# A hybrid layer on one core: attention blocks turned by row halves, reciprocals spread behind the values, and two small moves around the MLP

## The chip, the cores and the metric

The kernel runs on one core of a Trainium2 chip. A core has a matrix engine (PE, whose weight loads the profile lists apart as PEld), a vector engine (DVE), a scalar engine (ACT), a general engine (POOL), a queue engine (SP) that starts the transfers, and 16 DMA engines. Matrix products read from the on-chip memory of 128 partitions and write to eight banks of a second memory (PSUM), from which DVE and ACT copy results away. The metric is device time in microseconds of one execution, the median of several runs.

## The reference

One layer of a decoder on an input of 1024 positions and 1024 features, in float32. After a norm, one input projection feeds two mixers side by side: a gated delta rule (four heads of 128, chunks of 64) and a dilated attention (eight heads of 64). Their outputs go through one output projection and are added to the input. A norm, an up projection to 2 × 2816 columns, a causal convolution of width 3, a gate, a down projection and a final norm follow. Of the attention:

```python
def band_attention(q, k, v, n_back):          # query l sees keys l-n_back..l
    ...
    s = jnp.einsum('...nqd,...nkd->...nqk', qb, kk)
    ...
    m = jnp.max(s, axis=-1)
    p = jnp.exp(s - m[..., None])
    den = jnp.sum(p, axis=-1)
    num = jnp.einsum('...nqk,...nkd->...nqd', p, vv)

def dilated_attention(q, k, v):
    for window, dil in ((128, 1), (512, 4), (2048, 16)):
        ...                                   # band attention over the keys at stride dil
    ...
    num_tot = wts[0][..., None] * nums[0] + wts[1][..., None] * nums[1] + wts[2][..., None] * nums[2]
    out = num_tot / den_tot[..., None]
```

and of the end of the layer:

```python
    h = rmsnorm(x, norm2_w)
    u = causal_dwconv(h @ w_up, ffn_conv_w)
    gate, up = u[..., :D_FF], u[..., D_FF:]
    x = x + (jax.nn.silu(gate) * up) @ w_down
    ...
    return rmsnorm(x, final_norm_w)
```

## The kernel before

Large products are made of three products of a rounded high part and a low part (`mm3`: high·high, low·high, high·low); in the rows they are `xhi,whi`, `xlo,whi`, `xhi,wlo`, each 128 x 512. The up and down projections are made of seven products instead of eight blocks (`P1` to `P7` in `up`), on sums and differences of the operands' blocks.

**Order of the work.** The kernel is written as generators, one for each strand: the norm and gates, the dense input projection, eight chains of the delta rule, the attention, the output projection, the MLP. A planner (`Weave`, lines 46 to 118) runs them in turn. It keeps an estimated time of PE and of when each tile is ready; a strand yields how long it would have to wait (`need`), and another strand's products are put in its place. What comes out is one fixed order of all PE instructions, which is stamped on them. The order on DVE and ACT is made by a scheduler from the program order and two priorities: `uv` and `ua` are the urgent handles of DVE and ACT, `ve` and `ac` the plain ones. So a product of the attention stands between products of the dense projection, and where its operand is late, PE waits, whatever could be done behind it.

**The attention** (lines 892 to 1045) takes two heads at a time (`e` = 0, 1, in partitions 0 to 63 and 64 to 127), four head pairs `pi`, two halves `hh` of the positions, and in each half two pairs of 128-row blocks (`u` = 0, 1 and 2, 3). The function `advance` does one such pair a step: it turns the pair before, computes this pair's scores, and finishes the pair before.

- `scores` (line 904): products of `kT,qT`, by row halves for the near keys (64*128) and in sixteenths for the dilated ones (64*32), into banks `asc` and `atr`, two of each. `softmax` (929): DVE takes maximum and mask into `sm`, ACT the exponential with its sum `den`.
- `turn` (942): DVE writes `rd`, the reciprocal of `den` over 128 x 128. Then each 128 x 128 block of `sm` is transposed on PE (`tp`, line 192, `ps<-ident,sm` with L193), for each head into one bank of `asc` or `atr`. DVE copies the near blocks to `pt`, ACT the dilated ones to `pb`. The next scores use the same banks.
- `spread` (966): PE transposes the two `rd` of a pair into a bank, so that the reciprocals lie along the free dimension. At the end of a half ACT copies the bank to `rT`.
- `values` (975): `pt,vn`, by column halves (128*64). `merge_classes` (984): `pb,vc` for the dilated keys. `give` (998): DVE multiplies the bank of values by `rT` into `oT`, and SP sends it to the mixer's memory.

In the rows an entry such as 64*128 is the part of the 128 x 128 array that an instruction uses, rows by columns.

**The passage to the up projection** (`up`, lines 1246 to 1288, for the first column block, where `before is None`). PE computes P1, P5, three quarters of P2, P6, the last quarter of P2; then `rms2_power` (1174) sums the squares of the second norm with `ones` and has DVE and POOL make the reciprocal roots `rs`; then P7, then `rms2_spread` (1183): eight transpositions of `rs` into two banks, copied by DVE to `rstdB`; then P4. ACT copies the banks of P1, P6 and P7 to `p1`, `u2`, `u3` (rows `p<-pa`, `u<-pa`), beside splitting weights (`S`, `pair`).

**The last product** (`last_product` 1485, `complete` 1421, `final_norm` 1430). The last rows of the down projection end in two halves of 256 columns. For each, DVE adds to `x1h`, ACT squares it, DVE adds the square to `rstdB`; then PE sums `rstdB` over the partitions with `ones`, POOL makes the reciprocal root, PE spreads it, DVE scales and SP writes out.

Of the kernel before, what the change touches and what calls it, by code (L numbers as in the profile page):

```python
# [15 lines left out]
P = 128  # L16
# [128 lines left out]
def hybrid_layer(tc, I, out):  # L145
# [43 lines left out]
        tc.stamp_issue_order_token(nc.tensor.matmul(dst, lhs, rhs, start=start, stop=stop, **kw).ins, TOKEN)  # L189
        wv.product(us, dst, lhs, rhs)  # L190

    def tp(dst, src):
        tc.stamp_issue_order_token(nc.tensor.transpose(dst, src, ident).ins, TOKEN)  # L193
        wv.product(0.11, dst, src)

    def mm3(dst, lhs, rhs, first, last, **kw):
        us = 0.2135 * rhs[0].shape[-1] / 512
# [694 lines left out]
    def attention():  # L892
# [47 lines left out]
            it["den"] = den  # L940

        def turn(pair):
            pts = A("pt", "dv*", shape=(P, 4, 256))
            for b, (it, tag) in enumerate(zip(pair, ("asc", "atr"))):
                sm, near, far, den, u = it["sm"], it["near"], it["far"], it["den"], it["u"]
                rd = tile_(sp, [P, P], F32, "rd", ("r0", "r1", "w0", "w1")[u], 1)
                uv.reciprocal(rd.rearrange("p (e d) -> p e d", e=2), den[:, :, None].to_broadcast([P, 2, 64]))
                it["rd"] = rd
                nf = -(-far // P)
                it["pt"] = []  # L950
                for e in range(2):
                    pt = pts[:, 2 * b + e, :]
                    it["pt"].append(pt)
                    pp = bank(tag)
                    yield wv.need(pp, sm, slack=TSLACK[b])
                    for i in range(near // P):
                        tp(pp[:, i * P:(i + 1) * P], sm[:, e, far + i * P:far + (i + 1) * P])
                    for i in range(nf):
                        tp(pp[:, near + i * P:near + (i + 1) * P], sm[:, e, i * P:(i + 1) * P])
                    uv.tensor_copy(pt[:, :near], pp[:, :near])  # L960
                    for i in range(nf):
                        rows = min(far - i * P, P)
                        ua.activation(it["pb"][e][:rows, it["u"], i, :], pp[:rows, near + i * P:near + (i + 1) * P],
                                      AF.Copy)

        def spread(pair):
            g = pair[0]["g"]
# [5 lines left out]
                ac.activation(g["rT"], g["rb"], AF.Copy)  # L973

        def values(pair):
            yield wv.need(pair[0]["po"], *pair[0]["pt"], slack=-PSLACK)
            for it in pair:
                u = it["u"]
                for i in range(it["near"] // P):
                    for e, er in enumerate(HALVES):  # L980
                        mm(it["po"][er, u * P:(u + 1) * P], v8(it["vn"])[:, it["k0"] // P + i, er],
                           it["pt"][e][:, i * P:(i + 1) * P], 0.11, u == 0 and i == 0, False, skip_group_check=True)

        def merge_classes(g):
            vcv = g["vc"].rearrange("p (b c d) -> p b c d", b=2, c=4)
            po, hh = g["po"], g["hh"]
            yield wv.need(*g["pb"], slack=-PSLACK)


            parts = (((0, 128, 0), (1, 64, 2)) if hh else ((0, 64, 2),))  # L990
            for b, rows, u in parts:
                for c in range(4):
                    for e, er in enumerate(HALVES):
                        mm(po[er].rearrange("p (u t) -> p u t", u=4)[:, u:, 32 * c:32 * c + 32],
                           vcv[:rows, b, c, er], g["pb"][e][:rows, u:, b, 32 * c:32 * c + 32], 0.11 - 0.028 * u,
                           False, c == 3 and b == hh, skip_group_check=True)

        def give(g):
# [14 lines left out]
        def advance(pair):  # L1013
            done = pipe.pop() if pipe else None
            if done is not None:
                yield from turn(done)
            if pair is not None:
                yield from scores(pair)
                pipe.append(pair)
            if done is not None:  # L1020
                yield from spread(done)
                yield from values(done)
                if done[1]["u"] == 3:
                    yield from merge_classes(done[0]["g"])
                    give(done[0]["g"])

        for pi in range(4):
            q, k, vn, vc = cur
            for hh in range(2):
                if hh == 1 and pi < 3:  # L1030
                    yield from wv.until(("a", pi + 1, 1))
                    cur = att_load(pi + 1)
                po = bank("ch")
                pb = [A("pb", "qa", shape=(P, 4, 1 + hh, P)) for _ in range(2)]
                if pi == 3 and hh == 1:
                    wv.done.add("last group")
                for t in pb:
                    for rows, b in (((slice(96, 128), 0), (slice(32, 64), 1)) if hh else ((slice(32, 64), 0),)):
                        po_.memset(t[rows, 0 if b < hh else 2, b, :], 0.0)
# [206 lines left out]
    def up(n, before):  # L1246

        xg, xu = A("xg", "kT"), A("xu", "kT")
        pa = bank("asc", "pa")
        yield from up_product(n, "P1", pa, True, False)  # L1250
        p1 = tile_(sp, [P, 512], F32, "p1", "t2", 2)
        ac.activation(p1, pa, AF.Copy)
        if before is not None:
            yield from before()
        pc = bank("ch", "pc")
        if before is None:

            yield from up_product(n, "P5", pc, True, False)
            pd = bank("hf", "pd")
            yield from up_product(n, "P2", pd, ks=range(3))  # L1260
        yield from up_product(n, "P6", pa, False, False)
        u2 = tile_(wp, [P, 512], F32, "u2", "wlo", 2)
        ac.activation(u2, pa, AF.Copy)
        if before is None:
            yield from up_product(n, "P2", pd, False, ks=(3,))
            rs = rms2_power()
        else:
            yield from up_product(n, "P5", pc, True, False)
        yield from up_product(n, "P7", pa, False, False)
        if before is None:  # L1270
            rms2_spread(rs)
        else:
            pd = yield from next_bank("hf")
            yield from up_product(n, "P2", pd)
        u3 = tile_(sp, [P, 512], F32, "u3", "t2", 2)
        ac.activation(u3, pa, AF.Copy)
        ve.tensor_tensor(xu[:, half(1)], u3, pc, op=OP.add)
        ve.tensor_tensor(xg[:, half(0)], p1, pd, op=OP.add)
        yield from up_product(n, "P4", pa, False, True)
        ac.activation(xu[:, half(0)], pa, AF.Copy)  # L1280

        def rest():
            yield from up_product(n, "P3", pc, False)
            ve.tensor_tensor(xg[:, half(1)], u2, pc, op=OP.add)
            del W[n]
            up_tail(n, xg, xu)
        ve.tensor_tensor(xu, xu, rstdB, op=OP.mult)
        last["rest"] = rest
# [129 lines left out]
        x = x1h[m][:, part(m, hh, sl)]  # L1418
        ve.tensor_tensor(x, x, pd[:, sl], op=OP.add)

    def complete(m, hh, sl):

        sp_ = part(m, hh, sl)
        x = x1h[m][:, sp_]
        sq = tile_(sp, [P, 512], F32, "sq3", "t2", 2)
        ac.activation(sq[:, sl] if m else rstdB[:, sp_], x, AF.Square)
        if m:
            ve.tensor_tensor(rstdB[:, sp_], rstdB[:, sp_], sq[:, sl], op=OP.add)

# [24 lines left out]
    def mlp_down():  # L1454
# [117 lines left out]
```

## Time and profile before

| | |
|---|---|
| median of 3 runs | 1228.7 us (1227.79 to 1230.6) |
| the profiled execution | 1227.88 us |
| its span in the trace | 1226.0 us |
| PE busy | 1205.9 us, 98% |
| PEld busy | 992.4 us, 81% |
| DVE busy | 948.6 us, 77% |
| ACT busy | 574.7 us, 47% |
| POOL busy | 53.2 us, 4% |
| `ps<-ident,sm` on PE | 184 instructions, 23.9 us |
| `ps<-pt,vn` / `ps<-pb,vc` on PE | 240, 16.6 us / 192, 9.6 us |

A row of a group reads: line, engine, operation, tiles (output, then operands), shape in the array and form, count; then busy us, mean ns of one; then the idle time of the engine just before them and what ended it. Matrix products overlap, so the start of one to the start of the next is the time that it takes, and the duration of one is longer than that. In rows in order of time the first number is the start in the span, the second the length of the row's work together, and the count stands at the end. Line 189 is the helper of all products, 193 that of all transpositions, 139 and 141 those of the plain and the urgent instructions of DVE and ACT; so groups are told apart by their tiles.

### The profile page before, as it was taken

To read this page: it belongs to the slowest core of one execution; us is meant where nothing else is said; L and a number is where in the kernel's file an instruction comes from. 1 tells how busy PE (TensorE), PEld (TensorE's weight loads), DVE (VectorE), ACT (ScalarE), POOL (GpSimd) and SP (SyncE) were. 2 spreads that over 40 slices of the span, in tenths; PEclk is the share of its full clock that TensorE was granted. 3 is DMA by queue.
4 is the path that set the end of the run, shared out by engine and by line. 5 is a ranking of instruction groups with operands and counts; after the bars stand their busy time and mean duration, and the time that the engine had idled before them with its cause. 6 is when DMAs were issued, how large, how long until landed. Compare 5 with 4: busy or idle time off the path is not lost.

```text
span 1226.0 us, 17889 instructions
## 1 busy us (share of the span) xinstructions
PE 1205.9 (98%) x6880; PEld 992.4 (81%) x6880; DVE 948.6 (77%) x1458; ACT 574.7 (47%) x1123; POOL 53.2 (4%) x58
## 2 busy tenths in 40 slices
PE   9999999999999999999999999999999999999996
PEld 7878887888777777788788888888888888787886
DVE  7675964566477686667888989889888889898875
ACT  7393344256344453555545445444454453344441
POOL 0211010003100000000000000000000000000000
PEclk9999999999999999999999999999999999999998
DMA  7425252345733213444123132231322397455623
GB/s 232 104 87 157 84 152 74 121 137 151 225 104 113 80 36 89 165 151 152 52 88 103 52 103 82 74 103 52 103 88 68 122 366 256 166 168 172 193 86 138
DMA packets 85799, 154.79 MB, mean 126 GB/s; under 512 B 21169, under 2 KB 36305, under 8 KB 85713
## 3 DMA queue, kind: packets, MB, share of 16 engines
q1 hardware_dynamic: 85712, 153.64, 39.0%
q8 instruction: 54, 0.88, 0.3%
q14 instruction: 33, 0.26, 0.1%
HBM read 117.68 MB, written 35.93 MB: 125 GB/s over the span
## 4 chain that ended last, share of the span: by engine, by line
PE 82%; DVE 8%; DMA 4%; issue 2%; ACT 2%; POOL 0%; SPq 0%; POOLq 0%; DVEq 0%; ACTq 0%
PE ps L189 43%; PE pa L189 19%; PE pc L189 10%; PE dw L189 8%; PE ps L193 3%; DMA wd<-in_wd 2%; DVE pr L139 2%; DVE x1h L139 1%; DVE wd L139 1%; DVE kT L139 1%; ACT dec L139 1%; DMA xt<-in_xT 1%; DVE wlo L139 0%; DMA wst<-in_wu 0%; DVE r L139 0%
## 5 line engine op out<-in xcount | busy, mean ns | idle before, releaser
L189 PE MATMUL dw<-pr 128*128 128x512 f32 (+1 forms) x984 | 213.4, 377 | 2.9 <-DVE x1h L139 2.5
L189 PEld LDWEIGHTS dw<-pr 128*128 128x128 f32 x984 | 176.0, 188 | 39.2 <-DVE x1h L139 4.7
L189 PE MATMUL ps<-xhi,whi 128*128 128x512 f32 x384 | 158.6, 413 | 0.0
L189 PE MATMUL ps<-xlo,whi 128*128 128x512 f32 x384 | 149.9, 390 | 0.4 <-DVE xlo L139 0.4
L189 PE MATMUL ps<-xhi,wlo 128*128 128x512 f32 x384 | 150.3, 391 | 0.0
L189 PE MATMUL pa<-T,pair 128*128 128x512 f32 x528 | 127.1, 389 | 0.6 <-ACT u L139 0.6
L189 PEld LDWEIGHTS pa<-T,pair 128*128 128x128 f32 x528 | 98.9, 188 | 21.1 <-ACT u L139 0.6
L189 PEld LDWEIGHTS ps<-xhi,wlo 128*128 128x128 f32 x384 | 72.0, 188 | 15.8 <-DVE wlo L139 0.2
L189 PEld LDWEIGHTS ps<-xhi,whi 128*128 128x128 f32 x384 | 72.3, 188 | 15.2 <-issue 2.6
L189 PEld LDWEIGHTS ps<-xlo,whi 128*128 128x128 f32 x384 | 72.4, 189 | 12.5 <-DVE xlo L139 0.8
L139 ACT ACTIVATE whi<-wst 128x1024 fp32r<-128x1024 f32 (+2 forms) x42 | 43.0, 1023 | 82.0 <-PE ps L189 68.1
L139 ACT ACTIVATE u<-pa 128x512 f32<-128x512 f32 x44 | 26.3, 599 | 110.6 <-PE pa L189 110.6
L139 DVE SCALAR_TENSOR_TENSOR y<-xu,fcw,y 128x1023 f32<-128x1023 f32 (+1 forms) x44 | 56.4, 1281 | 25.7 <-ACT y L139 25.6
L189 PE MATMUL pa<-B,A 128*128 128x512 f32 x264 | 63.4, 389 | 0.0
L189 PE MATMUL pa<-T,S 128*128 128x512 f32 x264 | 63.4, 389 | 0.0
L189 PE MATMUL pc<-B,pair 128*128 128x512 f32 x264 | 63.4, 389 | 0.0
L189 PE MATMUL pc<-T,S 128*128 128x512 f32 x264 | 63.4, 389 | 0.0
L139 DVE TENSOR_TENSOR wst<-wst 128x512 f32<-128x512 f32 x88 | 60.5, 687 | 0.8
L189 PE MATMUL ps<-B,pair 128*128 128x512 f32 x252 | 60.5, 389 | 0.0
L139 DVE TENSOR_TENSOR wlo<-wst,whi 128x1024 fp32r<-128x1024 f32 (+2 forms) x42 | 49.4, 1177 | 13.6 <-ACT whi L139 13.5
L139 ACT ACTIVATE pr<-wd 128x1024 fp32r<-128x1024 f32 x33 | 34.9, 1059 | 50.7 <-DVE wd L139 24.8
L141 ACT ACTIVATE sm<-sm,mx 128x128 f32<-128x128 f32 (+7 forms) x64 | 35.5, 557 | 48.1 <-DVE mx L141 48.1
(240 smaller groups left out, 2371.0 us busy)
## 6 DMA issues: line engine op xcount, KB each, us to landing
wst<-in_wu SPq DMA_DIRECT2D x44, 512.0 KB, 3.7
wd<-in_wd SPq DMA_DIRECT2D x44, 512.0 KB, 4.0
upark<-y SPq DMA_DIRECT2D x22, 512.0 KB, 3.7
wst<-in_wi SPq DMA_DIRECT2D x21, 512.0 KB, 3.7
r<-upark SPq DMA_DIRECT2D x11, 512.0 KB, 7.9
r<-upark SPq DMA_DIRECT2D x22, 256.0 KB, 7.2
wa<-in_wd SPq DMA_DIRECT2D x22, 256.0 KB, 2.7
wst<-in_wv SPq DMA_DIRECT2D x8, 512.0 KB, 3.6
```

The costliest lines, as they stand in the source:

```text
L139: return getattr(eng, op)(*a, **kw)
L141: return getattr(eng, op)(*a, **kw)
L189: tc.stamp_issue_order_token(nc.tensor.matmul(dst, lhs, rhs, start=start, stop=stop, **kw).ins, TOKEN)
L193: tc.stamp_issue_order_token(nc.tensor.transpose(dst, src, ident).ins, TOKEN)
```

## The change

There are four parts.

1. `turn` transposes each 128 x 128 block in two pieces, one for each half of the rows (64 partitions by 128 columns), with the 64 x 64 identity of the same rows. The piece of the upper rows goes to one bank and that of the lower rows to another. 184 transpositions in 128*128 become 368 in 64*128. A bank now holds both heads of one row half; a copy takes the near blocks of both heads for one row half (`pt`), or one dilated block of both heads (`pb`). There are as many copies as before. `pb` is laid out anew, with 12 memsets by POOL instead of 24. The reciprocal `rd` is written behind the copies in the program.
2. In `advance`, `values` and `merge_classes` come ahead of `spread`, and `give` is last. With it the copy `rT` comes later on ACT.
3. In the first `up`, the bank copies `p1`, `u2`, `u3` are urgent instructions of ACT, and `rms2_spread` moves from between P7 and P4 to behind P4.
4. In the last half of the last product, the square of the last row block isn't added to `rstdB` by DVE; PE sums it as a second product into the same bank.

```diff
-    def tp(dst, src):
-        tc.stamp_issue_order_token(nc.tensor.transpose(dst, src, ident).ins, TOKEN)
-        wv.product(0.11, dst, src)
+    def tp(dst, src, idt=None, us=0.11):
+        tc.stamp_issue_order_token(nc.tensor.transpose(dst, src, ident if idt is None else idt).ins, TOKEN)
+        wv.product(us, dst, src)
...
         def turn(pair):
-            pts = A("pt", "dv*", shape=(P, 4, 256))
+            pts = A("pt", "dv*", shape=(P, 2, 2, 256))
             for b, (it, tag) in enumerate(zip(pair, ("asc", "atr"))):
-                sm, near, far, den, u = it["sm"], it["near"], it["far"], it["den"], it["u"]
-                rd = tile_(sp, [P, P], F32, "rd", ("r0", "r1", "w0", "w1")[u], 1)
+                sm, near, far, u, den = it["sm"], it["near"], it["far"], it["u"], it["den"]
+                nn, nf = near // P, -(-far // P)
+                pt = it["pt"] = pts[:, b]
+                pps = [bank(tag) for _ in range(2)]
+                yield wv.need(*pps, sm, slack=TSLACK[b])
+                pvs = [pp.rearrange("p (e i t) -> p e i t", e=2, t=64) for pp in pps]
+                for e in range(2):
+                    for i in range(nn + nf):
+                        o = far + i * P if i < nn else (i - nn) * P
+                        for pv, rr in zip(pvs, HALVES):
+                            tp(pv[:, e, i, :], sm[rr, e, o:o + P], ident[rr, rr], 0.055)
+                for pv, rr in zip(pvs, HALVES):
+                    uv.tensor_copy(pt.rearrange("p e (i t) -> p e i t", t=P)[:, :, :nn, rr], pv[:, :, :nn, :])
+                    for i in range(nf):
+                        rows = min(it["far"] - i * P, P)
+                        ua.activation(it["pb"][i][:rows, :, u, rr], pv[:rows, :, nn + i, :], AF.Copy)
+                rd = it["rd"] = tile_(sp, [P, P], F32, "rd", ("r0", "r1", "w0", "w1")[u], 1)
                 uv.reciprocal(rd.rearrange("p (e d) -> p e d", e=2), den[:, :, None].to_broadcast([P, 2, 64]))
-                it["rd"] = rd
-                nf = -(-far // P)
-                it["pt"] = []
-                for e in range(2):
-                    pt = pts[:, 2 * b + e, :]
-                    it["pt"].append(pt)
-                    pp = bank(tag)
-                    yield wv.need(pp, sm, slack=TSLACK[b])
-                    for i in range(near // P):
-                        tp(pp[:, i * P:(i + 1) * P], sm[:, e, far + i * P:far + (i + 1) * P])
-                    for i in range(nf):
-                        tp(pp[:, near + i * P:near + (i + 1) * P], sm[:, e, i * P:(i + 1) * P])
-                    uv.tensor_copy(pt[:, :near], pp[:, :near])
-                    for i in range(nf):
-                        rows = min(far - i * P, P)
-                        ua.activation(it["pb"][e][:rows, it["u"], i, :], pp[:rows, near + i * P:near + (i + 1) * P],
-                                      AF.Copy)
...
             if done is not None:
-                yield from spread(done)
                 yield from values(done)
                 if done[1]["u"] == 3:
                     yield from merge_classes(done[0]["g"])
+                yield from spread(done)
+                if done[1]["u"] == 3:
                     give(done[0]["g"])
...
-                pb = [A("pb", "qa", shape=(P, 4, 1 + hh, P)) for _ in range(2)]
+                pb = [A("pb", "qa", shape=(P, 2, 4, P)) for _ in range(1 + hh)]
...
-        ac.activation(p1, pa, AF.Copy)
+        copy = (ua if before is None else ac).activation
+        copy(p1, pa, AF.Copy)
...
-        ac.activation(u2, pa, AF.Copy)
+        copy(u2, pa, AF.Copy)
...
         yield from up_product(n, "P7", pa, False, False)
-        if before is None:
-            rms2_spread(rs)
-        else:
+        if before is not None:
...
-        ac.activation(u3, pa, AF.Copy)
+        copy(u3, pa, AF.Copy)
...
         yield from up_product(n, "P4", pa, False, True)
         ac.activation(xu[:, half(0)], pa, AF.Copy)
+        if before is None:
+            rms2_spread(rs)
...
+    squares = {}
...
-    def complete(m, hh, sl):
+    def complete(m, hh, sl, apart=False):
...
-        if m:
+        if apart:
+            squares["last"] = sq
+        elif m:
             ve.tensor_tensor(rstdB[:, sp_], rstdB[:, sp_], sq[:, sl], op=OP.add)
...
-            mm(ss[:, c:c + 1], rstdB[:, o:o + P], ones[:, :1], 0.215)
+            more = squares.get("last")
+            mm(ss[:, c:c + 1], rstdB[:, o:o + P], ones[:, :1], 0.215, True, more is None)
+            if more is not None:
+                mm(ss[:, c:c + 1], more[:, sl.start + c * P:sl.start + c * P + P], ones[:, :1], 0.215, False, True)
...
-            complete(4 + i, 0, sl)
+            complete(4 + i, 0, sl, sl.start > 0 and i == 3)
```

More of the change, by code (lines that the diff above doesn't have):

```diff
@@ L975, in values @@
         def values(pair):
-            yield wv.need(pair[0]["po"], *pair[0]["pt"], slack=-PSLACK)
+            yield wv.need(pair[0]["po"], pair[0]["pt"], slack=-PSLACK)
             for it in pair:
@@ L981, in values @@
                         mm(it["po"][er, u * P:(u + 1) * P], v8(it["vn"])[:, it["k0"] // P + i, er],
-                           it["pt"][e][:, i * P:(i + 1) * P], 0.11, u == 0 and i == 0, False, skip_group_check=True)
+                           it["pt"][:, e, i * P:(i + 1) * P], 0.11, u == 0 and i == 0, False, skip_group_check=True)
         def merge_classes(g):
@@ L994, in merge_classes @@
                         mm(po[er].rearrange("p (u t) -> p u t", u=4)[:, u:, 32 * c:32 * c + 32],
-                           vcv[:rows, b, c, er], g["pb"][e][:rows, u:, b, 32 * c:32 * c + 32], 0.11 - 0.028 * u,
+                           vcv[:rows, b, c, er], g["pb"][b][:rows, e, u:, 32 * c:32 * c + 32], 0.11 - 0.028 * u,
                            False, c == 3 and b == hh, skip_group_check=True)
@@ L1033, in attention @@
                 po = bank("ch")
-                pb = [A("pb", "qa", shape=(P, 4, 1 + hh, P)) for _ in range(2)]
+                pb = [A("pb", "qa", shape=(P, 2, 4, P)) for _ in range(1 + hh)]
                 if pi == 3 and hh == 1:
                     wv.done.add("last group")
-                for t in pb:
-                    for rows, b in (((slice(96, 128), 0), (slice(32, 64), 1)) if hh else ((slice(32, 64), 0),)):
-                        po_.memset(t[rows, 0 if b < hh else 2, b, :], 0.0)
+                for rows, b in (((slice(96, 128), 0), (slice(32, 64), 1)) if hh else ((slice(32, 64), 0),)):
+                    po_.memset(pb[b][rows, :, 0 if b < hh else 2, :], 0.0)
                 g = dict(po=po, pb=pb, hh=hh, pi=pi, vc=vc, rb=bank("ch"))
```

## The prediction

> **What bounds the kernel now.** Read first: the page's busy shares and the chain of work that ended last, then the attention's stretch in the table by windows (sum, then PE, PEld, DVE, ACT, POOL busy, granted clock, DMA share, GB/s).
>
> ```profile
> span 1226.0 us, 17889 instructions
> PE 1205.9 (98%) x6880; PEld 992.4 (81%) x6880; DVE 948.6 (77%) x1458; ACT 574.7 (47%) x1123; POOL 53.2 (4%) x58
> PE 82%; DVE 8%; DMA 4%; issue 2%; ACT 2%; POOL 0%; SPq 0%; POOLq 0%; DVEq 0%; ACTq 0%
> 329.00:460.00 131.00, 130.54 (x1358) 100.52 (x1355) 99.58 (x248) 60.90 (x204) 3.42 (x18) 1.00 0.29 88
> ```
>
> PE is the bound, 130.54 of 131.00 us even in the attention, at full clock. So PE time that is saved there ends the kernel earlier, unless a step of PE's written order then stands waiting for DVE or ACT, which are 76% and 46% busy. A busy PE also holds its own idle turns: the rows below start later than the work before them needs. I therefore count from start to start.
>
> Next the groups of the attention (kinds of operands kept apart: busy us, mean ns of one, idle before), and one stretch of PE in order of time (start, length, count at the end).
>
> ```profile
> L193 PE MATMUL ps<-ident,sm 128*128 128x128 f32 x184 | 23.9, 275 | 0.1
> L193 PEld LDWEIGHTS ps<-ident,sm 128*128 128x128 f32 x184 | 20.8, 141 | 3.1 <-ACT sm L141 1.1
> L189 PEld LDWEIGHTS ps<-kT,qT 64*128 64x128 f32 x128 | 10.7, 186 | 6.8 <-issue 3.6 <-ACT pb L141 2.3 <-DVE pt L141 0.4
> L189 PEld LDWEIGHTS ps<-pb,vc 64*64 64x64 f32 x128 | 4.4, 134 | 1.4 <-issue 1.4
> L189 PEld LDWEIGHTS ps<-kT,qT 64*32 64x32 f32 x384 | 4.2, 106 | 4.0 <-issue 4.0
> ```
> ```profile
> 341.89 0.39 PE L189 MATMUL ps<-xhi,wlo 128*128 128x512 f32 x1
> 342.21 1.68 PE L189 MATMUL ps<-kT,qT 64*128 64x256 f32 x40
> 343.82 0.44 PE L193 MATMUL ps<-ident,rd 128*128 128x128 f32 x2
> 344.19 1.09 PE L189 MATMUL ps<-pt,vn 128*64 128x128 f32 x16
> 345.21 0.68 PE L189 MATMUL ps<-pb,vc 64*64 64x64 f32 x16
> 345.82 0.50 PE L189 MATMUL ps<-xhi,whi 128*128 128x512 f32 x1
> 346.16 0.39 PE L189 MATMUL ps<-xlo,whi 128*128 128x512 f32 x1
> 346.38 0.39 PE L189 MATMUL ps<-xhi,wlo 128*128 128x512 f32 x1
> 346.62 1.47 PE L193 MATMUL ps<-ident,sm 128*128 128x128 f32 x12
> 347.84 0.48 PE L189 MATMUL ps<-xhi,whi 128*128 128x512 f32 x1
> 348.16 0.40 PE L189 MATMUL ps<-xlo,whi 128*128 128x512 f32 x1
> ```
>
> From these rows: twelve transpositions take (1.47 − 0.273)/11 = 0.109 us each, and no more around them: 346.62 to 348.16 is 1.54 = 12 × 0.109 + 0.23, and 0.23 is what a dense product takes (346.16 to 346.38, 0.22). A burst in another shape of the array does cost more. The reciprocals, 343.82 to 344.19, take 0.37 for two times 0.109: 0.15 too much. The values, 344.19 to 345.21, take 1.02 for eight pairs of 0.109: 0.15 too much. The classes (`pb,vc`) and the first dense product after them take 0.95, 345.21 to 346.16. Eight pairs fit in what 16 instructions of 0.68 leave, about 0.058 a pair, so 0.95 is 0.47 + 0.23 + 0.25; and before such a burst 0.09 is lost (341.89 to 342.21 instead of 0.23). A burst in another shape between dense products therefore costs about 0.35.
>
> **The change, part by part.**
>
> *Turning by row halves.* 184 transpositions become 184 pairs, one for each row half, each moving 64 columns instead of 128. No row has such a pair. Three rows are near. In the scores two row halves run side by side: two of them together end in 0.49, each being 0.48 long.
>
> ```profile
> 419.93 0.49 PE L189 MATMUL ps<-kT,qT 64*128 64x256 f32 x2
> ```
>
> The classes move 64 columns a pair in 0.058. And loading: by the rows above, 32, 64 and 128 columns take 106, 134 and 186 ns, but the 128 columns of a transposition 141, little more than 64 columns of another product. So its load fits into 58 ns as well. I take 0.058 a pair: 184 × (0.109 − 0.058) = −9.4 us. Bounds: 0.109, if the load of a half takes as long as the row of `kT,qT` has it (64 columns more cost 186 − 134 = 52 ns, so 128 of them some 104), which saves nothing; 0.116, if the two halves follow each other, which adds 1.3.
>
> Against it stands the shape: the turns leave 128*128. The new written order has 17 bursts of them, at 0.35 each: +5.95 us.
>
> The DVE copies (64) and the ACT copies (64) keep their number and elements; the halves of one block are filled alternately, so in a burst of twelve the first copy can start after six pairs, 6 × 0.058 = 0.35 us, instead of three transpositions, 3 × 0.109 = 0.33. I cost this at nothing; the copies start behind DVE's reciprocals anyway (below), and with pairs of 0.109 they would be 0.3 later. POOL's memsets halve; POOL is 3.42 us busy in the whole stretch, so nothing. The SP queue keeps its DMAs.
>
> *Reciprocals behind the values.* `rd` stood between scores and values, a 128*128 island between two other shapes. Behind the values it lies beside dense products, where 128*128 costs nothing extra. Sixteen islands × 0.15 to 0.2: −2.75 us. What it delays: `rT` on ACT comes behind the next four exponentials, and `oT` with its DMA waits for it; out of the way of PE, except through DVE's order in the third step below.
>
> PE alone: −9.4 + 5.95 − 2.75 = −6.2 us. A head pair runs four steps, with 6, 12, 12 and 16 transpositions; per step PE saves 0.13, 0.43, 0.43 and 0.64 (51 ns each, less 0.35, plus 0.17 for the island), four times.
>
> Now what is late next. In the third step DVE sets the pace (DVE, ACT and PE in order of time):
>
> ```profile
> 415.92 0.95 DVE L141 RECIPROCAL rd<-mx 128x128 f32<-128x128 f32 x1 [0.40 <-ACT sm L141]
> 416.44 1.47 PE L193 MATMUL ps<-ident,sm 128*128 128x128 f32 x12
> 416.79 1.05 DVE L139 TENSOR_TENSOR oT<-ps,rT 128x512 f32<-128x512 f32 x1
> 417.68 0.92 DVE L141 RECIPROCAL rd<-mx 128x128 f32<-128x128 f32 x1
> 418.52 1.35 DVE L141 COPY pt<-ps 128x256 f32<-128x256 f32 x4
> 418.98 1.20 ACT L141 ACTIVATE pb<-ps 96x128 f32<-96x128 f32 x4 [1.89 <-DVE pt L141]
> ```
>
> The next scores, at 419.93 (row above), need the banks that `pt` empties until 419.87. The reciprocals and `oT` stand ahead of the copies in the new order too, so this chain begins and ends where it did: four times 0.43 is gained by PE and lost in waiting. In the fourth step ACT or DVE sometimes is as close; of one such place the trace has the wait already:
>
> ```profile
> 390.00 0.76 DVE L141 COPY pt<-ps 128x256 f32<-128x256 f32 x2
> 390.94 1.03 PE L189 MATMUL ps<-kT,qT 64*128 64x256 f32 x4 [0.32 <-ACT pb L141]
> ```
>
> I count two of the four fourth steps as lost (1.2) and 0.2 for the small first bursts. Attention: −6.2 + 1.7 + 1.4 = −3.1 us. Its bounds are −6.2 (nothing held) and 0 (all held).
>
> *Passage to the up projection* (PE, ACT, POOL):
>
> ```profile
> 586.68 3.02 PE L189 MATMUL pa<-T,pair 128*128 128x512 f32 x12 [0.55 <-ACT u L139]
> 588.56 2.00 POOL L139 TENSOR_TENSOR rs<-rs,mhalf 128x8 f32<-128x8 f32 x1 [155.09 <-DVE rs L139]
> 589.51 1.06 ACT L139 ACTIVATE pair<-wst 128x1024 fp32r<-128x1024 f32 x1 [0.94 <-PE pa L189]
> 590.47 0.58 ACT L139 ACTIVATE u<-pa 128x512 f32<-128x512 f32 x1
> 590.62 1.09 PE L193 MATMUL ps<-ident,rs 128*128 128x128 f32 x8 [0.92 <-POOL rs L139]
> 591.46 3.00 PE L189 MATMUL pa<-T,pair 128*128 128x512 f32 x12
> ```
>
> PE waits for POOL's power until 590.57, turns `rs` eight times and starts P4 at 591.46. With the turns behind P4, P4 waits only for `u3` (the bank copy at 590.47, ending 591.05). In the new order the copies `u2` and `u3` stand on ACT where they stood, so being urgent gains nothing: `u3` still stands behind the `pair` of 589.51. P4 starts at 591.1, 0.36 earlier, and the eight turns, 8 × 0.109 = 0.87, come behind it: +0.5 us. Bounds: −0.9 (ACT takes `u3` first after all) and +1.0. The DVE work on `rstdB` moves behind P4 and has 3 us of P3 as cover.
>
> *Last squares summed by PE* (DVE, PE):
>
> ```profile
> 1215.55 0.95 DVE L139 TENSOR_TENSOR rstdB<-rstdB,sq 128x256 f32<-128x256 f32 x2 [0.21 <-ACT sq L139]
> 1216.65 0.58 PE L189 MATMUL ps<-ones,rstdB 128*128 128x1 f32 x4 [2.10 <-DVE rstdB L139]
> ```
>
> The second of two additions of 0.42 goes, so PE starts at about 1216.12 instead of 1216.65; it issues four passes more, (0.58 − 0.25)/3 = 0.11 each: −0.53 + 0.45 = −0.1 us.
>
> Sum: −3.1 + 0.5 − 0.1 = −2.7 us.
>
> **The rivals.**
>
> *A half's load lasts as long as a whole one's* (the slower side). Its place is every pair of the turn, its price the 0.35 of 17 bursts with nothing to pay for it: +5.95 − 2.75 + 0.5 − 0.1 = +3.6 us, 1232.3. It decides from 0.09 us a pair upwards (184 × 0.019 = 3.5 saved is then what the rest costs). For it: the load of `kT,qT`'s halves, 186. Against it: the transposition's own 141. [...]
>
> *The copies hold everything.* All four steps are paced by DVE and ACT; PE's gain turns into waits ahead of the scores. For it: the third step and 390.94. Against it: the second and fourth steps, where ahead of the scores dense products run without idle time. 0 + 0.5 − 0.1: 1228.7 to 1229.2.
>
> *Nothing is held*: −6.2 + 0.5 − 0.1 = −5.8, 1222.9. For it: DVE has 31 us free in the stretch; against it the row of 415.92 to 419.87.
>
> **How the numbers follow.** The profiled execution took 1227.88 us, 1.88 beside its span; the median of the runs is 1228.7. The sum against the profiled one gives 1225.2, against the median 1226.0; I give 1225.7, as the holds of the fourth step are the roughest term. Pairs at 0.058 with some held: chance 0.60, own range 1222.5 to 1227.5. All held: 0.18. Load in full: 0.22. A measurement of this kernel tells about 0.2%, 2.46 us, from no change: faster is under 1226.2, slower above 1231.2. Of the first case 0.48 is faster, of the second 0.03; slower are 0.19 of the third and 0.04 of the second (the whole 5.95 of switching not paid back where copies hold); the rest, 0.26, is the same. The range: 1221.7 (all of PE's gain, and 1 us in the passage) to 1231.8, which takes in the second case and leaves out most of the third.
>
> **What would show it.** Right: `ident,sm` as 368 of 64*128, sixteen pairs within 1.2 us; `ident,rd` directly before a dense product; the attention from its first scores to its last values about 3 us shorter; new waits of PE for `pt` ahead of the third step's scores; P4 at once behind P7 but for `u3`, eight turns of `rs` behind P4. Wrong: pairs 0.1 us apart; a burst's switch over 0.5; or waits for copies ahead of all scores.

## The result and the profile after

The changed kernel takes 1226.26 us (median of 20 runs, 1223.94 to 1228.53) beside 1228.68 (20 runs): a ratio of 0.9977, 95% interval 0.9972 to 0.9983. That is 2.4 us by the medians, where 3.0 were forecast (1225.7). The profiled execution took 1227.22 us, so it lies above the median, and its span is only 0.6 us below the one before.

The same rows of the changed kernel: the page's shares, the groups of the turn on PE and PEld, and PE in order of time.

```profile
span 1225.4 us, 18242 instructions
PE 1204.1 (98%) x7068; PEld 988.6 (81%) x7068; DVE 949.5 (77%) x1457; ACT 574.8 (47%) x1123; POOL 49.6 (4%) x46
```
```profile
L193 PE MATMUL ps<-ident,sm 64*128 64x64 f32 x368 | 15.8, 228 | 0.6
L193 PEld LDWEIGHTS ps<-ident,sm 64*128 64x128 f32 x368 | 13.0, 139 | 6.4 <-ACT sm L141 4.8 <-issue 1.6
```
```profile
347.81 0.44 PE L193 MATMUL ps<-ident,rd 128*128 128x128 f32 x2
348.00 0.48 PE L189 MATMUL ps<-xhi,whi 128*128 128x512 f32 x1
...
348.55 0.40 PE L189 MATMUL ps<-xhi,wlo 128*128 128x512 f32 x1
348.88 0.97 PE L193 MATMUL ps<-ident,sm 64*128 64x64 f32 x24
349.77 0.50 PE L189 MATMUL ps<-xhi,whi 128*128 128x512 f32 x1
350.11 0.40 PE L189 MATMUL ps<-xlo,whi 128*128 128x512 f32 x1
```

The load of a half takes 139 ns, as the whole transposition's did (141), and the halves run side by side: the two of a pair start 3 to 8 ns apart, and twelve pairs take 0.89 us from start to start. Of that, about 0.14 is the change of shape at both ends, which leaves 0.062 a pair. From 348.55 to 350.11, with the dense product ahead and the slow start of the next (0.34 instead of 0.23), 1.56 us pass where 1.78 passed in the kernel before, so a burst of twelve saves 0.22. The reciprocals (`rd`) now cost 0.19, less than two turns' time, since they lie beside the dense products.

The whole attention, from its first scores to the start of the last `xhi,whi` product of the input projection, which is the same work in all kernels, read by windows (sum, then PE, PEld, DVE, ACT, POOL busy, granted clock, DMA share, GB/s); first the kernel before, then the changed one:

```profile
328.70:483.86 155.16, 154.70 (x1500) 120.47 (x1500) 113.35 (x262) 68.58 (x213) 3.42 (x18) 1.00 0.27 82
```
```profile
329.95:481.08 151.13, 150.03 (x1684) 113.75 (x1684) 113.71 (x262) 68.59 (x213) 2.43 (x8) 1.00 0.29 84
```

4.03 us shorter. Two things gave most of it back in this execution. The attention began 1.25 us later (329.95 instead of 328.70), and the passage to the up projection lost 2.1 us (from the first sum of squares to P1 of the next column block 12.08 us instead of 10.01). Here are PE and ACT in the passage of the changed kernel, then two windows of it with the granted clock (the column behind POOL), and last the row of P1 in the kernel before:

```profile
581.51 1.84 PE L189 MATMUL ps<-ones,rstdB 128*128 128x1 f32 x16
583.46 0.58 ACT L141 ACTIVATE u<-pa 128x512 f32<-128x512 f32 x1
584.09 4.47 PE L189 MATMUL pa<-T,pair 128*128 128x512 f32 x12 [0.73 <-ACT u L141]
588.36 1.06 ACT L139 ACTIVATE pair<-wst 128x1024 fp32r<-128x1024 f32 x1 [2.39 <-PE pa L189]
589.32 0.58 ACT L141 ACTIVATE u<-pa 128x512 f32<-128x512 f32 x1
589.95 3.01 PE L189 MATMUL pa<-T,pair 128*128 128x512 f32 x12 [1.40 <-ACT u L141]
592.80 1.03 PE L193 MATMUL ps<-ident,rs 128*128 128x128 f32 x8
593.59 2.99 PE L189 MATMUL pa<-B,A 128*128 128x512 f32 x12
```
```profile
583.40:584.00 0.60, 0.00 (x0) 0.00 (x0) 0.60 (x2) 0.60 (x2) 0.00 (x0) 0.83 0.00 0
584.10:587.40 3.30, 3.30 (x8) 2.63 (x9) 3.21 (x6) 1.58 (x2) 1.43 (x1) 0.53 0.00 0
```
```profile
594.30 2.88 PE L189 MATMUL pa<-B,A 128*128 128x512 f32 x12
```

P7 (584.09) waits for the bank copy `u2`, as it did before, and then runs at a granted clock of 0.50 until 587.21: 4.47 us instead of 3.02. P4 follows `u3`, which still stands behind a `pair`, and the eight turns of `rs` (transpositions that lay the reciprocal roots along the free dimension) come behind P4, as forecast. From P7's first product to P1 of the next column block (`pa<-B,A`), 9.50 us pass, in the kernel before 7.62 (586.68 to 594.30).

At the end DVE adds one square less and PE starts earlier:

```profile
1215.10 0.43 DVE L139 TENSOR_TENSOR rstdB<-rstdB,sq 128x256 f32<-128x256 f32 x1 [0.21 <-ACT sq L139]
...
1218.27 3.22 DVE L139 SCALAR_TENSOR_TENSOR x1h<-x1h,fw,ps 128x256 f32<-128x256 f32 x8 [1.30 <-PE ps L193]
```

From the start of these additions (two before, one now) to the first scaling: 1215.10 to 1218.27 is 3.17 us, before 1215.55 to 1218.80, 3.25. That is the 0.1 of the forecast, in this pair of traces.

### The profile page after: what moved, and what is told of

Same layout as the page of the kernel before. It is cut to its first block, busy times and chain, and to the rows that moved or that the text cites. A ratio compares the mean times of both kernels' runs of the same rounds, so it can differ in the third digit from the quotient of the medians.

```text
span 1225.4 us, 18242 instructions
## 1 busy us (share of the span) xinstructions
PE 1204.1 (98%) x7068; PEld 988.6 (81%) x7068; DVE 949.5 (77%) x1457; ACT 574.8 (47%) x1123; POOL 49.6 (4%) x46
## 4 chain that ended last, share of the span: by engine, by line
PE 88%; DVE 6%; issue 2%; ACT 2%; DMA 1%; SPq 0%; POOLq 0%; POOL 0%; DVEq 0%; ACTq 0%
PE ps L189 43%; PE pa L189 19%; PE dw L189 13%; PE pc L189 10%; PE ps L193 3%; DVE pr L139 1%; DVE x1h L139 1%; DVE kT L139 1%; DMA wd<-in_wd 1%; PE warm L189 1%; ACT dec L139 1%; DMA wst<-in_wu 0%; DVE wlo L139 0%; ACT sq L141 0%; DMA r<-upark 0%
## 5 line engine op out<-in xcount | busy, mean ns | idle before, releaser
L189 PEld LDWEIGHTS pc<-T,S 128*128 128x128 f32 x264 | 49.5, 188 | 10.3
```

## The experiments

The questions: which part gave the attention's 4 us; what the third part costs; and where the low clock comes from. The fourth part wasn't run alone.

**Each of the first two parts alone.** `halves_only` is the kernel before with the new `turn` (and its layouts of `pt` and `pb`). Against the changed kernel its edit is this, and the third and fourth part are taken back too:

```diff
             if done is not None:
+                yield from spread(done)
                 yield from values(done)
                 if done[1]["u"] == 3:
                     yield from merge_classes(done[0]["g"])
-                yield from spread(done)
-                if done[1]["u"] == 3:
                     give(done[0]["g"])
```

> The kernel before with the first part alone: blocks turned by row halves, reciprocals still spread ahead of the values, passage and tail as before. Theory (the row halves pay by themselves): 184 pairs, now seen at 0.062 us each, save 184 x (0.109 - 0.062) = 8.6 us of PE, 18 bursts in another shape cost 0.35 each = 6.3 us, so about -2.3 us: 1226.4. Steps C and D of each head pair shorter by 0.25 to 0.45 us, step A longer. Rival (what the attention gained comes from the spread behind the values, which also takes the rT copy out from between the exponentials): within 0.5 us of the kernel before, 1228.2 to 1229.2.

`spread_only` is the kernel before with this edit the other way round (`values` and `merge_classes` ahead of `spread`) and nothing else.

> The kernel before with the second part alone: values and classes ahead of the spread of the reciprocals. Theory: the sixteen 128*128 islands of 0.15 to 0.2 us go, -2.75 us: 1225.9. Rival (only the 0.17 of each island goes where PE and not a copy ends the step): -1 us or less, 1227.7. If the rT copy mattered, the third step of a head pair is the one that gets shorter by more than 0.2 us.

Measured: `halves_only` 1224.3 us, ratio 0.9965 (0.9952 to 0.9977); `spread_only` 1226.65, ratio 0.9980 (0.9970 to 0.9990). The same stretch of the attention, first with the halves alone, then with the spread alone:

```profile
328.83:481.45 152.62, 151.98 (x1684) 114.27 (x1684) 113.21 (x262) 67.90 (x213) 2.43 (x8) 1.00 0.27 83
```
```profile
328.60:481.24 152.64, 151.96 (x1500) 120.28 (x1500) 113.87 (x262) 68.89 (x213) 3.41 (x18) 1.00 0.27 83
```

2.54 and 2.52 us shorter than 155.16: each pays by itself, by about the sums of its bursts and islands (-2.3 and -2.75), and the rival that one of them does it all falls. Together they give 4.03, one less than the sum. The third steps show that nothing is held there. From their scores to the next scores, before 342.21 to 350.11, 7.90; with the halves, then with the spread:

```profile
343.45 1.68 PE L189 MATMUL ps<-kT,qT 64*128 64x256 f32 x40
351.15 1.94 PE L189 MATMUL ps<-kT,qT 64*128 64x256 f32 x40
```
```profile
342.10 1.68 PE L189 MATMUL ps<-kT,qT 64*128 64x256 f32 x40
349.80 1.89 PE L189 MATMUL ps<-kT,qT 64*128 64x256 f32 x40
```

7.70 both, and 7.50 in the changed kernel: 0.20 each, and they add. Counted without the dense products between, what is missing from the sum lies in the first steps of the four head pairs (about 0.8 us, the next experiment) and in the fourth ones (about 0.3). The time of `halves_only` fell by more than its attention; its trace is 2.0 us shorter in the down projection too (215.4 us from the first product to the last, before 217.4), which this part doesn't touch. That stage takes 215.4 to 219.4 us in the fourteen traces, so I take those 2 us for scatter between executions, and the times below scatter with it.

**Small blocks turned whole.** The first step of each head pair became longer in the changed kernel. `small_whole` (the changed kernel without its third part) turns the two blocks without dilated keys as before:

```diff
...
+                if not nf:
+                    for e in range(2):
+                        pp = bank(tag)
+                        yield wv.need(pp, sm, slack=TSLACK[b])
+                        for i in range(nn):
+                            tp(pp[:, i * P:(i + 1) * P], sm[:, e, i * P:(i + 1) * P])
+                        uv.tensor_copy(pt[:, e, :near], pp[:, :near])
+                else:
+                    yield from halves(it, tag, pt, b)
```

> The changed kernel with the passage undone, and the first two blocks of a head pair (no dilated keys) turned whole, as in the kernel before. Theory (a burst in another shape costs 0.35 us whatever is in it, and six pairs save 6 x 0.047 = 0.28): step A of each head pair, longer by 0.1 to 0.4 us in the changed kernel, gets 0.1 to 0.4 shorter, 0.8 us over three or four pairs: 1222.2. Rival (step A is held by copies, not by PE): unchanged, 1223.0.

Measured: 1224.52 us, ratio 0.9961 (0.9947 to 0.9974). From the first scores to the second ones, the first step took 6.56 before (328.70 to 335.26). The changed kernel, then this one:

```profile
329.95 0.93 PE L189 MATMUL ps<-kT,qT 64*128 64x128 f32 x8
...
336.89 1.32 PE L189 MATMUL ps<-kT,qT 64*128 64x256 f32 x15
```
```profile
329.89 0.93 PE L189 MATMUL ps<-kT,qT 64*128 64x128 f32 x8
...
336.46 0.91 PE L189 MATMUL ps<-kT,qT 64*128 64x256 f32 x5
```

6.94 becomes 6.57, with the same dense products between: two small bursts, of two and four pairs, in another shape cost more than their six pairs save. In the other three head pairs, where the six pairs form one burst, the first step got 0.04 to 0.07 shorter, so in all it is worth about 0.5 us, too little for the times to show.

**The passage.** `passage_undone` is the changed kernel with its third part taken back (plain `ac` for `p1`, `u2`, `u3`, the turns of `rs` between P7 and P4). It ran twice.

> The changed kernel with the third part undone: bank copies not urgent, rs spread between P7 and P4 as before. In the changed kernel's trace the passage lost 1.9 us against the kernel before: some 1.4 in P7, whose products ran at a granted clock of 0.50, and 0.5 by the order. Theory A (the lowered clock comes with the changed order): the whole 1.9 us comes back, 1224.4. Theory B (it comes from the wait ahead of P7, which is the same in both orders once the attention ends earlier): P7 runs slow here too, and only 0.5 us comes back, 1225.8.

> The changed kernel with the passage undone, once more, for its time beside the run with the passage mended and for a second trace. Theory (the third part costs 0.5 us by its order): 1224.0 to 1225.5, 0.5 to 1.5 below the changed kernel. Rival (its first time, 1223.0, was the true one, and the third part costs 3 us): 1222.5 to 1223.5. In the trace, P7's first product to P1 of the next block takes 7.4 to 7.6 us in both.

`after_again` is the changed kernel, unaltered.

> The changed kernel once more, unaltered, for a second trace. In the first one the transfer of the next weights (second wst of in_wu) landed 4.3 us after its issue, in the three traces without a wait ahead of P7 3.3 to 3.5 us, with the same order on ACT. Theory (the landing varies between executions, and the bank copy u2 stands behind the splits of these weights): this trace can have either; if the split begins 3.5 us or less after the issue, P7 follows the sums of squares at once and at full clock, and the span is 1.9 us shorter than before, near 1223.5. Rival (the changed order itself makes the landing late or the clock low): 4.2 us, a wait of 0.7 or more ahead of P7 and a clock of 0.5 again.

Measured: `passage_undone` 1223.01 us (six runs), ratio 0.9955 (0.9940 to 0.9970), and at the second time 1225.62 (twelve runs), 0.9972 (0.9962 to 0.9982). `after_again` 1225.35, 0.9976 (0.9965 to 0.9986). The PE rows of `after_again`, with the ACT row that splits the first block of the next weights:

```profile
576.62 0.63 ACT L139 ACTIVATE A<-wst 128x512 fp32r<-128x512 f32 x1 [2.35 <-DMA wst<-in_wu]
...
583.31 3.06 PE L189 MATMUL pa<-T,pair 128*128 128x512 f32 x12
587.77 3.01 PE L189 MATMUL pa<-T,pair 128*128 128x512 f32 x12 [1.41 <-ACT u L141]
...
591.41 0.93 PE L189 MATMUL pa<-B,A 128*128 128x512 f32 x3
```

No wait ahead of P7 and full clock (1.00 over 580.00:594.00), with the same program. The split `A` starts when its transfer has landed. That transfer was issued at 571.41 and took 5.2 us; in the first trace it took 6.0 (571.36 to 577.38), and `A` started at 577.40. (The 3.3 to 4.3 us of the expectations are counted from the issue of the transfer behind it, at 573.14 and 573.09; the difference is the same.) On ACT the order is `A`, further splits, `u2`, and `u2` too starts 0.8 us later in the first trace. So the wait ahead of P7 is that of a transfer for the next block. `passage_undone` had an early landing in its first trace (5.0 us, no wait ahead of P7) and a late one in its second (6.0 us, a wait of 0.69, P7 in 3.01 us). Order alone is compared from P7 to the next P1: 7.44 and 7.61 with the passage undone, 7.62 before, 8.10 in `after_again`. The third part costs 0.5 to 0.7 us. The clock, 1.4, came on top in one of the two traces of the changed kernel. The two times of `passage_undone` differ by more than that, so the times can't tell the 0.5; neither theory about the sum (1.9 or 0.5 always) holds.

**The clock.** `gap_filled` puts four products of 128x512 ahead of P7:

```diff
             rs = rms2_power()
+            dummy = bank("atr")
+            for _ in range(4):
+                mm(dummy, B["T1"][0][0][:, :P], B["T1"][0][0], 0.2135)
```

> The changed kernel with four products of 128x512 into a spare bank put into PE's wait of 0.98 us ahead of P7; their result is not used. Theory (the idle time behind sixteen passes of one column lowers the clock): P7 starts when it did, its twelve products take 2.8 us instead of 4.3 at full clock, and the time falls by 1.4 us to 1224.9. Rival (the lowered clock is a matter of the single execution or of the one-column passes alone): P7 is slow again or the time is 1226.3 within 0.5 us.

Measured: 1225.14 us, 0.9970 (0.9959 to 0.9981), P7 in 2.88 us. This proves nothing: the transfer landed early (5.1 us after its issue), so there was no wait to fill. To have a wait in every execution, `gap_longer` writes `u2` three times, and `gap_longer_filled` has twelve products in the wait besides.

```diff
         copy(u2, pa, AF.Copy)
         if before is None:
+            for _ in range(2):
+                copy(u2, pa, AF.Copy)
```

> The changed kernel with the bank copy u2 written three times, so that PE waits longer ahead of P7 in every execution. The run with the filled gap did not test the clock, since its transfer landed early. Theory (idle time of more than 0.9 us behind the sixteen one-column passes lowers the clock): PE waits 2 to 4 us ahead of P7, and P7's products come 0.43 us apart at a granted clock of 0.5 for some microseconds. Rival (the one low clock seen was a matter of that execution): products 0.23 apart, clock 1.0.

> The same with twelve products of 128x512 into a spare bank in that wait, 2.8 us of work whose result is not used. Theory: with at most 1 us idle left, and that behind dense products, the clock stays at 1.0 and P7's products come 0.23 apart. Rival: low again, so the idle time is not the cause.

One execution each: 1230.16 and 1229.28 us, beside 1227.53 of the kernel before. PE's windows ahead of P7 and in P7 (the clock is the column behind POOL), first with the empty wait, then with the filled one:

```profile
583.50:586.50 3.00, 0.00 (x0) 0.00 (x0) 2.75 (x6) 2.97 (x6) 0.37 (x1) 0.56 0.00 0
586.70:590.20 3.50, 3.50 (x8) 2.77 (x9) 1.07 (x1) 0.00 (x0) 1.42 (x1) 0.50 0.37 95
```
```profile
583.60:586.40 2.80, 2.80 (x14) 2.15 (x13) 2.54 (x6) 2.77 (x6) 0.00 (x0) 1.00 0.00 0
587.00:590.00 3.00, 3.00 (x12) 2.17 (x12) 1.10 (x1) 0.18 (x1) 1.45 (x1) 1.00 0.28 67
```

With at least 3.0 us of idle time P7's products run at 0.50; with work in the wait, at 1.00. So it is the idle time ahead of P7 that goes with the low clock, as far as one execution of each can show. Its length alone hardly decides: 0.73 us went with half the clock in the first trace, 0.55 in the kernel before with the full one (1.00 over 580.00:594.00), and 0.69 in the second trace of `passage_undone` with P7 in 3.01 us, where the kernel before took 3.02. (The expectations count these waits 0.25 longer, from the start of the last one-column product.) The last section takes this up.

**The copies really first.** In the changed kernel the urgent handle left `u2` and `u3` where they had stood on ACT. `copies_forced` orders them by hand:

```diff
+            s1 = split_block(w["S1"], u0)          # next block's weights
+            if n == 1:
+                after(s1, last["u2"])
...
+            p1 = split_block(pairs[1], u)
+            if n == 1:
+                after(p1, last["u3"])
...
+            for t in last["late"]:                 # the last splits of T4 and B22
+                after(t, c2)
```

> The changed kernel with the two bank copies really put first on ACT: u2 ahead of the splits that wait for the next weights, u3 ahead of the second pair. Theory: P7 starts as soon as the sums of squares have been issued, whatever the transfer does, and P4 about 0.9 us after P7's last product instead of 1.9; no lowered clock. From the changed kernel -1.0 for u3, and -0.5 to -1.9 for u2 by how often the transfer is late: 1223.5 to 1224.8. Rival (the weights' splits, pushed back by 0.6 us each, make P1 of the next column block wait): no gain, 1226.

Measured: 1225.13 us, 0.9962 (0.9948 to 0.9975). `u2` now runs at once, and P7 follows the sums of squares although the transfer took 6.1 us to land. But P4 gains nothing, since `u3` stands behind the splits `S` and `pair`, and `S` waits 1.65 us for DVE's step on the same weights:

```profile
581.19 0.60 ACT L141 ACTIVATE u<-pa 128x512 f32<-128x512 f32 x1 [1.41 <-PE pa L189]
585.91 0.63 ACT L139 ACTIVATE S<-wst 128x512 fp32r<-128x512 f32 x1 [1.65 <-DVE wst L139]
586.45 1.04 ACT L139 ACTIVATE pair<-wst 128x1024 fp32r<-128x1024 f32 x1
587.39 0.58 ACT L141 ACTIVATE u<-pa 128x512 f32<-128x512 f32 x1
```

`forced_rs_ahead` adds the old place of the turns (`rms2_spread(rs)` between P7 and P4).

> As the run with the forced copies, and the eight turns of rs between P7 and P4 again, as in the kernel before: they cover the bank copy u3 if rs is ready by then. Theory: P7 starts at once; POOL's power is done within 0.3 us of P7's end, the turns take 0.87 and P4 follows without a wait: from P7's first product to P1 of the next block 6.6 to 7.0 us, where the changed kernel took 9.5 and the kernel with the passage undone 7.4. Time 0.5 to 0.8 below that with the passage undone: 1222.4. Rival: rs comes as late as before, PE waits 0.8 for POOL again, and the time is that with the passage undone, 1223.0.

Measured: 1223.28 us, 0.9955 (0.9943 to 0.9968); the rival came about, PE waits 1.1 us for POOL, because DVE starts `rs` behind its part of these splits. P7 to the next P1: 7.75. `passage_best` mends this too:

```diff
+        after(last["late"][1][1], last["rs"])      # DVE: rs ahead of B22's and S1's low parts
...
+            p0 = split_block(pairs[0], g)
+            if n == 1:
+                after(p0[0], last["u3"])           # ACT: u3 ahead of both pairs
```

> The changed kernel with the passage's order mended in three places: u2 on ACT ahead of the splits of the next weights, u3 ahead of both their pairs, DVE's step that starts rs ahead of those splits, and the turns of rs between P7 and P4 again. Theory (the passage's waits are all behind the splits of the next column block): no wait ahead of P7 and none for POOL, from P7's first product to P1 of the next block 6.5 us where the traces so far took 7.4 to 9.5, and the span of the passage 0.9 us shorter than with the passage undone; time 1222.3 to 1223.3. Rival (the splits pushed back delay P1 or P6 of the next block): the 0.9 us appears as a wait of the products behind P1, and the time is that with the passage undone, 1223.0 to 1224.

Measured: 1223.23 us, 0.9951 (0.9935 to 0.9967), the lowest ratio of all that ran, though its interval overlaps those of most other variants.

```profile
583.29 3.01 PE L189 MATMUL pa<-T,pair 128*128 128x512 f32 x12
586.36 1.09 PE L193 MATMUL ps<-ident,rs 128*128 128x128 f32 x8
587.35 3.01 PE L189 MATMUL pa<-T,pair 128*128 128x512 f32 x12
590.20 1.98 PE L189 MATMUL pa<-B,A 128*128 128x512 f32 x8
```

No wait for ACT or POOL is left that the profile names; P7 to the next P1 takes 6.91 us, 0.5 to 0.7 less than with the passage undone, and not the 0.9 expected.

## Why the prediction was right, and where it wasn't

- *The pair*: 0.058 forecast, 0.062 measured. The reason given for it, the load of a transposition being short, holds for its halves (139 ns), and the rival of the full load falls. A half's load did last as long as a whole one's (139 and 141 ns), but it doesn't set the pace here: from 348.93 on a pair comes every 62 ns, and the loads overlap.
- *The shape*: 0.35 a burst. Measured around the burst at 348.88: 0.10 ahead, 0.05 at its first pair, 0.09 behind and 0.11 in the next product, 0.35.
- *The islands of reciprocals*: -2.75 forecast, -2.52 by `spread_only`.
- *PE alone*: -6.2; with 0.062 a pair it would have been -5.4. The attention gave -4.03.
- *The third step held by DVE* was wrong: 0.43 was to be lost in each, and 0.40 was gained. I took the end of the last `pt` copy as the moment that releases the scores. But in the kernel before, the scores at 419.93 came 0.32 us behind the dense product ahead of them (419.61), as those at 342.21 did behind theirs (341.89): that is the change of shape, and no wait. In the changed kernel the scores begin before the copies end:

```profile
414.93 0.95 DVE L141 RECIPROCAL rd<-mx 128x128 f32<-128x128 f32 x1
416.00 0.58 ACT L139 ACTIVATE rT<-ps 128x512 f32<-128x512 f32 x1
417.85 1.39 DVE L141 COPY pt<-ps 128x256 f32<-128x256 f32 x4
419.02 0.49 PE L189 MATMUL ps<-kT,qT 64*128 64x256 f32 x2
```

 The copies end at 419.24, the scores start at 419.02. The scores write bank by bank, and the first two copies of `pt` and of `pb` have ended by 418.89; that each product waits for its own bank alone is my reading of this, and no run tests it. The chain also got shorter by itself, since `rT` left the exponentials (414.74 before, between them; now behind the last): the first reciprocal starts 3.40 us after the scores (411.53), before 3.88.
- *Two of the four fourth steps lost* was wrong too: the three that can be read are 0.45 to 0.48 shorter, of 0.64.
- *The first steps* are where the gain went that PE alone promised: instead of 0.13 saved each, they came 0.38, 0.32 and 0.12 longer and 0.07 shorter, counted without the dense products that the planner moved in or out. `small_whole` explains the first of them; of the second and third it took away 0.04 and 0.07, and their rest isn't settled. The attention's -3.1 was thus right in kind, with errors of opposite sign: too much lost in the third and fourth steps, too little in the first.
- *The passage*: +0.5 by order, measured 0.5 to 0.7. That `u3` would stay behind the `pair` was right. What was missed is that `u2` waits for a transfer of the next weights whose landing differs by 1 us from one execution to the next (5.0 to 6.1 us after its issue), and that in the first trace of the changed kernel the clock fell to 0.50 at this wait: 1.4 us more.
- *The tail*: -0.1, measured -0.08, with the clock at 1.00 in both (3.17 us in the first trace of the changed kernel, 3.25 in the kernel before).
- *Not foreseen*: in both traces of the changed kernel the attention begins 1.25 and 1.35 us later (below). It makes up for the attention's larger gain: -4.0 + 1.3 + 0.6 - 0.1 = -2.2 without the low clock, where -3.1 + 0.5 - 0.1 = -2.7 was forecast. That the total came out so near is luck in part.

## What to carry to other kernels

Before a step is called held by another engine, look which bank or buffer its first instruction needs, not when the last of a row of copies ends. In this kernel a copy that frees a bank stood behind what its engine was given earlier (`u3` at 589.32, behind a `pair` from 588.36), and a priority didn't change that order: read the order that was made, and look there for work of the next stage that waits for a transfer. Halving small transpositions pays only where a burst has enough of them: at the 0.35 us a burst and 0.047 saved a pair of this kernel, eight.

## What the runs showed of the hardware

PE's clock fell to half in the passage of two traces. In the first one of the changed kernel it fell at 583.79, 0.44 us after the last one-column product had ended (581.51 + 1.84), and rose at 587.21: 1.00 over 583.40:583.79, 0.50 over 583.79:587.21. With `gap_longer` it was 0.56 over 583.50:586.50, which puts the fall at about 583.86 (an estimate: 0.36 us at full clock, the rest at half), and still 0.50 over 586.70:590.20. So the long wait wasn't needed for the fall; with it the clock stayed low longer, at least 6.3 us by these figures instead of 3.42. What sets the moment of the fall, no run here tells.

One of DVE's operations on `kT` took 2.10 us instead of 1.27 when POOL's select had started 0.10 us ahead of it. The two groups ahead of the chains of the delta rule, kernel before, then changed:

```profile
51.59 2.71 DVE L139 SCALAR_TENSOR_TENSOR kT<-xr,gcw,kT 128x1023 f32<-128x1023 f32 x2
53.21 2.03 POOL L139 TENSOR_SCALAR_AFFINE_SELECT dec<-dec 128x1024 f32<-128x1024 f32 x1 [1.19 <-DMA dec<-gdram]
```
```profile
51.99 3.54 DVE L139 SCALAR_TENSOR_TENSOR kT<-xr,gcw,kT 128x1023 f32<-128x1023 f32 x2
53.33 1.12 POOL L139 TENSOR_SCALAR_AFFINE_SELECT dec<-dec 128x1024 f32<-128x1024 f32 x1 [0.90 <-ACT kT L139]
```

Before, the second DVE operation starts at 53.02, ahead of POOL, and takes 1.27, POOL's 2.03; in the changed kernel it starts at 53.43, behind POOL, and it is DVE's that is long (2.10, POOL's 1.12). The 0.83 us goes on through ACT to PE, which waits 0.91 at 69.7. It is two thirds of the 1.25 us; the other 0.40 stood already ahead of these rows (51.99 instead of 51.59). DVE's operation grew by 0.83, and 1.02 of POOL's was left when it started; by what one holds up the other no run here tells. The order of instructions up to there is the same in all kernels. In the traces of the kernel before, `halves_only` and `spread_only`, which lack one or both of the first two parts, the four operations on `kT`, of which the rows show the first two, take 6.76 us together; in both traces of the changed kernel and the first one of `passage_undone`, which have both parts, 7.59 to 7.60. What brings POOL's transfer in earlier against DVE's rows there stays open.
